# Layer 0's first norm, its values and its first queries and keys, made tile by tile of 128 features

## The chip, the core and the metric

The kernel runs on one core of one Trainium2 chip. The metric is the device time in microseconds of one execution of the whole program, the median of several runs; lower is better.

## The reference

256 tokens of 1024 features go through three layers: attention with a SwiGLU feed-forward, attention of another kind with a SwiGLU, and a convolution module with a convolutional feed-forward. Every sublayer is fed by a norm whose scale and shift come from a conditioning vector `c` through one large matrix (`ada_w`, 1024 x 6144 a layer).

```python
mod = (c_act @ ada_w[i] + ada_b[i])[:, None, :]
sh_a, sc_a, g_a, sh_f, sc_f, g_f = jnp.split(mod, 6, axis=-1)
h = rms_norm(x, norm_g[i, 0]) * (1.0 + sc_a) + sh_a
y = moba_attention(h, moba_w_qkv[i // 2], moba_w_o[i // 2], rel_bias)
x = x + g_a * rms_norm(y, norm_g[i, 1])
```

In layer 0 nothing can be projected before scale `sc_a` and shift `sh_a` are known. Each is a product of `c_act` with a 1024 x 1024 block of `ada_w`, 4 MB. The projections `h @ w_qkv` (1024 x 3072: queries, keys, values) follow.

## The kernel before

All weights stream from HBM once, in loads of 1 MB on SP's DMA queue (`load`, L74), into four buffers (`rawp`), and for the first three loads into tiles that other data uses later. A load can be issued when the last reader of its buffer is done. A weight unit is split into two pieces (`split`, L96): ACT copies it in the matrix engine's rounding (`h`, L108) and VectorE (DVE) subtracts that from the original (`l`, L110). Each product is three matmuls (`mm3`, L135 to L137). The activations `T` are split in the same way and stand with features on the partitions, in 8 tiles `k` of 128 features.

The first stretch of the program: `first_norm` (L284) loads the 8 MB of scale and shift in rows of 4 KB, multiplies them by `c_act` on the matrix engine (`quads`, L220), turns the two sums into columns, and scales the normed, transposed `x` by them. `project` (L207, first layer: `before=shifted`) makes the values V for all 256 tokens from four units of 1 MB. Then the loop of `attention` makes queries and keys for four pairs of heads, each from a unit of 1 MB (`cols_unit`, rows of 1 KB). While it does, the attention of the earlier heads is woven in (`step`): its first product is the scores matmul L615, which stands on the matrix engine's queue between the two blocks of pair 1's queries. Before that also stand the matmuls that turn the position bias (L375).

The other vectors of modulation are made in the background: `bg_step` takes a quarter of a vector (a load of 1 MB and two operations of 128x1024 on DVE, L202 and L204) at given places. The table `plans` says how many quarters a stage takes, over how many places, and how many places it leaves out first; layer 0's attention takes 12 quarters, and needs all of them at its end for the next norm.

A list scheduler sets the order in which the instructions stand on each engine's queue when the program is built; on the chip each queue runs strictly in that order.

## Time and profile before

| | us |
|---|---|
| median of 3 runs (lowest, highest) | 970.23 (968.81, 971.09) |
| profiled execution: first to last instruction | 967.0 |
| matrix engine (PE) busy | 928.9 |
| DVE busy | 767.5 |
| ACT busy | 495.1 |

The page gives the profiled execution's time from its first to its last instruction alone; the runs' median lies 3.2 us above it, which is what lies around the span. An engine is busy when one of its instructions runs; two matmuls overlap in the pipeline, so that PE's busy time says that it was fed, not that it was at its peak.

### The profile page before, as it was taken

To read this page: it belongs to the slowest core of one execution; us is meant where nothing else is said; L and a number is where in the kernel's file an instruction comes from. 1 tells how busy PE (TensorE), PEld (TensorE's weight loads), DVE (VectorE), ACT (ScalarE), POOL (GpSimd) and SP (SyncE) were. 2 spreads that over 40 slices of the span, in tenths; PEclk is the share of its full clock that TensorE was granted. 3 is DMA by queue.
4 is the path that set the end of the run, shared out by engine and by line. 5 is a ranking of instruction groups with operands and counts; after the bars stand their busy time and mean duration, and the time that the engine had idled before them with its cause. 6 is when DMAs were issued, how large, how long until landed. Compare 5 with 4: busy or idle time off the path is not lost.

```text
span 967.0 us, 17220 instructions
## 1 busy us (share of the span) xinstructions
PE 928.9 (96%) x6687; PEld 811.4 (84%) x6687; DVE 767.5 (79%) x1461; ACT 495.1 (51%) x870; POOL 51.2 (5%) x118
## 2 busy tenths in 40 slices
PE   5899999999999999999999999999999899999997
PEld 2579977998999879876799989987897779999996
DVE  1779977976878798887999878888777789977774
ACT  2355665543344445675634444555416755655552
POOL 2100000000000010122100000001000100000000
PEclk9999999999999999999999999999999999999999
DMA  9988885978879859673588899786747466975511
GB/s 349 390 318 293 316 283 176 322 283 317 282 272 382 300 185 348 225 259 106 167 285 320 311 345 336 275 303 204 269 113 201 142 208 226 302 231 188 175 45 44
DMA packets 141519, 244.06 MB, mean 252 GB/s; under 512 B 6662, under 2 KB 106174, under 8 KB 141438
## 3 DMA queue, kind: packets, MB, share of 16 engines
q1 hardware_dynamic: 140918, 241.64, 72.1%
q0 software_dynamic: 496, 1.31, 0.4%
q8 instruction: 52, 0.85, 0.4%
q14 instruction: 29, 0.24, 0.1%
q10 hardware_dynamic: 24, 0.01, 0.0%
HBM read 240.94 MB, written 2.01 MB: 251 GB/s over the span
## 4 chain that ended last, share of the span: by engine, by line
issue 44%; PE 30%; DVE 4%; POOL 4%; ACT 2%; DMA 1%; SPq 0%; DVEq 0%; POOLq 0%; ACTq 0%
PE up L137 5%; PE up L136 5%; PE up L135 5%; PE acc L135 4%; PE acc L137 4%; PE acc L136 4%; PE acc L851 1%; DVE l L110 1%; POOL rstd L480 1%; POOL var L478 1%; ACT h L108 1%; POOL orstd L652 1%; ACT junk L473 1%; POOL ovar L650 1%; DMA raw<-in_f_up_w_dram 1%
## 5 line engine op out<-in xcount | busy, mean ns | idle before, releaser
L110 DVE TENSOR_TENSOR l<-raw,h 128x512 fp32r<-128x512 f32 x548 | 354.7, 684 | 80.6 <-ACT h L108 78.2
L108 ACT ACTIVATE h<-raw 128x1024 fp32r<-128x1024 f32 x274 | 280.1, 1053 | 171.1 <-PE up L136 38.0
L137 PE MATMUL up<-th,l 128*128 128x256 f32 x640 | 181.7, 284 | 0.0
L136 PE MATMUL up<-tl,h 128*128 128x256 f32 x640 | 181.1, 283 | 0.0
L135 PE MATMUL up<-th,h 128*128 128x256 f32 x640 | 180.8, 282 | 0.0
L204 DVE SCALAR_TENSOR_TENSOR gemv<-raw,c_s,gemv 128x1024 f32<-128x1024 f32 x112 | 143.2, 1279 | 0.9
L135 PEld LDWEIGHTS up<-th,h 128*128 128x128 f32 x640 | 121.0, 189 | 2.0 <-DVE ml L747 0.4
L137 PEld LDWEIGHTS up<-th,l 128*128 128x128 f32 x640 | 120.7, 189 | 0.1
L136 PEld LDWEIGHTS up<-tl,h 128*128 128x128 f32 x640 | 120.4, 188 | 0.4
L135 PE MATMUL acc<-h,mh 128*128 128x512 f32 x232 | 91.6, 395 | 0.1
L136 PE MATMUL acc<-l,mh 128*128 128x512 f32 x232 | 90.9, 392 | 0.0
L137 PE MATMUL acc<-h,ml 128*128 128x512 f32 x232 | 90.5, 393 | 0.0
L137 PE MATMUL up<-oh,l 128*128 128x256 f32 x288 | 81.9, 284 | 0.0
L136 PE MATMUL up<-ol,h 128*128 128x256 f32 x288 | 81.7, 284 | 0.0
L135 PE MATMUL up<-oh,h 128*128 128x256 f32 x288 | 81.1, 282 | 0.0
L135 PE MATMUL acc<-th,h 128*128 128x256 f32 x256 | 75.1, 293 | 0.1
L137 PE MATMUL acc<-th,l 128*128 128x256 f32 x256 | 73.8, 288 | 0.2 <-DVE l L110 0.2
L136 PE MATMUL acc<-tl,h 128*128 128x256 f32 x256 | 72.7, 284 | 0.0
L135 PEld LDWEIGHTS up<-oh,h 128*128 128x128 f32 x288 | 54.6, 189 | 0.8
L136 PEld LDWEIGHTS up<-ol,h 128*128 128x128 f32 x288 | 54.2, 188 | 0.7
L137 PEld LDWEIGHTS up<-oh,l 128*128 128x128 f32 x288 | 54.4, 189 | 0.1
L135 PEld LDWEIGHTS acc<-h,mh 128*128 128x128 f32 x232 | 43.6, 188 | 11.1 <-issue 2.5
(230 smaller groups left out, 1663.7 us busy)
## 6 DMA issues: line engine op xcount, KB each, us to landing
raw<-in_ada_w_dram SPq DMA_DIRECT2D x46, 1024.0 KB
raw<-in_ffn_w_in_dram SPq DMA_DIRECT2D x36, 1024.0 KB
raw<-in_mod_w_dram SPq DMA_DIRECT2D x24, 1024.0 KB
raw<-in_ffn_w_out_dram SPq DMA_DIRECT2D x22, 1024.0 KB
raw<-in_f_up_w_dram SPq DMA_DIRECT2D x18, 1024.0 KB
raw<-in_moba_w_qkv_dram SPq DMA_DIRECT2D x12, 1024.0 KB
raw<-in_diff_w_qkv_dram SPq DMA_DIRECT2D x12, 1024.0 KB
raw<-in_f_down_w_dram SPq DMA_DIRECT2D x11, 1024.0 KB
```

Source lines behind the costliest of these rows:

```text
L108: newest["high"] = nc.scalar.activation(h, r, AF.Copy).ins
L110: newest["split"] = nc.vector.tensor_sub(l[:, k], r[:, k], h[:, k].bitcast(F32)).ins
L135: nc.tensor.matmul(ps, lh, rh, start=start, stop=False, skip_group_check=True)
L136: nc.tensor.matmul(ps, lh, rl, start=False, stop=False, skip_group_check=True)
L137: nc.tensor.matmul(ps, ll, rh, start=False, stop=stop, skip_group_check=True)
L204: nc.vector.scalar_tensor_tensor(t, src, c[:, k:k + 1], t, op0=ALU.mult, op1=ALU.add)
L473: nc.scalar.activation(junk, src, AF.Square, scale=1.0 / 32, accum_out=ss[:, i:i + 1])
L478: nc.gpsimd.tensor_scalar(v, ss[:, 0:1], ss[:, 1:2], EPS, op0=ALU.add, op1=ALU.add)
L480: nc.gpsimd.tensor_tensor(r, v, mhalf, op=ALU.pow)
L650: nc.gpsimd.tensor_scalar(var, ss, 1.0 / DH, EPS, op0=ALU.mult, op1=ALU.add)
L652: nc.gpsimd.tensor_tensor(rn, var, mhalf, op=ALU.pow)
L851: mm = nc.tensor.matmul(ps[32 * g:32 * g + 32, 0:P], lw[t][:, m, g, :], ur[:, g, 4 * m:4 * m + P], start=m == 0, stop=m == 7, tile_positio ...
```

## The change

Scale and shift of layer 0's first norm are made for 128 features at a time. For each of the 8 tiles one load of 1 MB takes the 128 columns of scale and the 128 of shift that belong to the tile: 2 x 1024 pieces of 512 bytes. The product with `c_act` is made on PE for tiles 0 to 2 (`FIRST_ON_PE`) and on DVE for tiles 3 to 7: one multiply and seven multiply-adds of 128x256 (new lines L337 and L339), then two matmuls with one column each (L342) and two small operations (L345, L347) that leave scale and shift as columns. ACT makes the tile of `T` with them (L349, L350), DVE its second piece (L351). As soon as a tile of `T` is there, its share of all values and of pair 0's queries and keys is added up in PSUM, 12 matmuls of 512 and 12 of 256 columns a tile. Pair 0's queries and keys come in two units with rows of 1 KB (`half_unit`). `x` is loaded first. The background's 12 quarters start in pair 1 (`plans`), 8 of them beside pairs 1 to 3 and 4 beside the output projection.

```diff
+    def first_columns():
...
+        rows = work.tile([24, P], F32, name="rowsm", tag="w")
+        w, b, c = jobs[0][0], jobs[0][1], jobs[0][5]
+        for i, v in enumerate((b[D:2 * D], b[0:D], jobs[0][3])):
+            nc.scalar.dma_start(rows[8 * i:8 * i + 8, :], v.rearrange("(k p) -> k p", p=P))
+        ps = tr.tile([P, 512], F32, name="tr")
+        nc.tensor.transpose(ps[:, 0:24], rows, ident[:24, :24])
+        col = one.tile([P, 24], F32, name="mcol")
+        nc.vector.tensor_copy(col, ps[:, 0:24])
+        nc.vector.tensor_scalar(col[:, 0:8], col[:, 0:8], 1.0, None, op0=ALU.add)
+        return col
...
+    def first_load(k):
+        w = jobs[0][0]
+        return load(lambda raw: [(raw[:, 1024 * i:1024 * i + 1024].rearrange("p (r n) -> p r n", r=8),
+                                  w[:, j * D + k * P:j * D + k * P + P].rearrange("(p r) n -> p r n", r=8))
+                                 for i, j in enumerate((1, 0))])
+    def first_tile(T, k, raw, col, on_pe):
+        c = jobs[0][5]
+        rows = raw.rearrange("p (j r n) -> p j r n", j=2, r=8)
+        g = work.tile([P, 2, P], F32, name="fgem", tag="w")
+        if on_pe:
+            ps = tr.tile([P, 512], F32, name="tr")
+            for r in range(8):
+                q = 32 * (r % 4)
+                nc.tensor.matmul(ps[q:q + 32, 0:256], c[:, r:r + 1].to_broadcast([P, 32]), rows[:, :, r, :],
+                                 start=r < 4, stop=r >= 4, tile_position=(0, q), skip_group_check=True)
+            nc.scalar.activation(g.rearrange("p j n -> p (j n)"), ps[:, 0:256], AF.Copy)
+        else:
+            nc.vector.tensor_scalar(g, rows[:, :, 0, :], c[:, 0:1], None, op0=ALU.mult)
+            for r in range(1, 8):
+                nc.vector.scalar_tensor_tensor(g, rows[:, :, r, :], c[:, r:r + 1], g, op0=ALU.mult, op1=ALU.add)
+        ps = tr.tile([P, 512], F32, name="tr")
+        for j in range(2):
+            nc.tensor.matmul(ps[:, j:j + 1], g[:, j, :], pick if on_pe else ones32[:, 0:1], start=True, stop=True,
+                             skip_group_check=True)
+        m = small.tile([P, 2], F32, name="fcols")
+        nc.vector.scalar_tensor_tensor(m[:, 0:1], ps[:, 0:1], col[:, k:k + 1], col[:, 16 + k:17 + k],
+                                       op0=ALU.add, op1=ALU.mult)
+        nc.vector.tensor_tensor(m[:, 1:2], ps[:, 1:2], col[:, 8 + k:9 + k], op=ALU.add)
+        v = work.tile([P, S], F32, name="fv", tag="w")
+        nc.scalar.activation(T[0][:, k, :], nb[:, k, :], AF.Identity, scale=m[:, 0:1], bias=m[:, 1:2])
+        nc.scalar.activation(v, nb[:, k, :], AF.Identity, scale=m[:, 0:1], bias=m[:, 1:2])
+        nc.vector.tensor_sub(T[1][:, k, :], v, T[0][:, k, :].bitcast(F32))
...
+    def first_project(w):
...
+        T = new_T("t")
+        col = first_columns()
+        turned = first_rows()
+        vals = [[acc.tile([P, 512], F32, name="acc") for _ in range(2)] for _ in range(2)]
+        qk = [up.tile([P, 512], F32, name="up") for _ in range(2)]
+        vw, qw = {}, {}
...
+        def values(k):
+            wh, wl = vw[k // 2][k % 2]
+            for h in range(2):
+                for n in range(2):
+                    sl = slice(512 * n, 512 * n + 512)
+                    mm3(vals[h][n], *tok(T, k, h), wh[:, sl], wl[:, sl], k == 0, k == NK - 1)
+        def heads(k):
+            wh, wl = (t[:, k % 2, :] for t in qw[k // 4][k // 2 % 2])
+            for i in range(2):
+                for b in range(2):
+                    sl = slice(256 * i + 128 * b, 256 * i + 128 * b + 128)
+                    mm3(qk[i][:, 256 * b:256 * b + 256], wh[:, sl], wl[:, sl], T[0][:, k, :], T[1][:, k, :],
+                        k == 0 and b == 0, k == NK - 1)
+        def tile_of(k):
+            first_tile(T, k, raws.pop(k), col, k < FIRST_ON_PE)
+        raws = {0: first_load(0)}
+        v0 = rows_load(w, 0, 2 * D)
+        raws[1] = first_load(1)
+        tile_of(0)
+        with tc.issue_after(turned):
+            make_c2()
+        vw[0] = split(v0, after=turned)
+        load_qk(0)
         for k in range(NK):
-            v = nb[:, k, :]
-            nc.vector.tensor_scalar(v, v, cols[0][:, k:k + 1], None, op0=ALU.mult)
...
+            if k + 2 < NK:
+                raws[k + 2] = first_load(k + 2)
+            if k + 1 < NK:
+                tile_of(k + 1)
+            if k % 2 == 0 and k + 2 < NK:
+                load_v(k // 2 + 1)
+            if k == 2:
+                load_qk(1)
+            values(k)
+            heads(k)
+        return T, qk, vals
...
@@ -661,14 +723,31 @@
     def attention(diff, T, w_qkv, w_o, first):
         v = big.tile([P, 2, D], F32, name="v")
-        for h, ps in project(T, w_qkv, 2 * D, ("oh", "ol"), before=first):
-            for n in range(2):
-                nc.scalar.activation(v[:, h, 512 * n:512 * n + 512], ps[n], AF.Copy)
+        pairs = []
+        scale = -float(DH // (2 if diff else 1)) ** -0.5
+        def pair(pq, pk):
+            q = two.tile([P, 2, S], F32, name="q")
+            nc.scalar.activation(q, pq.rearrange("p (b n) -> p b n", b=2), AF.Copy, scale=scale)
+            yield
...
+            nc.scalar.activation(kk, pk.rearrange("p (b n) -> p b n", b=2), AF.Copy)
+            pairs.append((q, kk))
         if first:
+            T, qk, vals = first_project(w_qkv)
+            for h, ps in enumerate(vals):
+                for n in range(2):
+                    nc.scalar.activation(v[:, h, 512 * n:512 * n + 512], ps[n], AF.Copy)
+            for _ in pair(*qk):
+                pass
             next(bias)
             lam_col()
+        else:
+            for h, ps in project(T, w_qkv, 2 * D, ("oh", "ol")):
+                for n in range(2):
+                    nc.scalar.activation(v[:, h, 512 * n:512 * n + 512], ps[n], AF.Copy)
         O = new_T("o")
...
             elif flight:
                 advance()
-        for i in range(4):
+        if first:
+            heads(0)
+        for i in range(len(pairs), 4):
             pq = acc.tile([P, 512], F32, name="acc")
...
             pk = acc.tile([P, 512], F32, name="acc")
+            made = pair(pq, pk)
...
+            next(made, None)
             heads(i)
         step()
...
     stages.append((2, 2, lambda T: conformer(T, a["a_pw1_w_2"][0], a["a_pw2_w_2"][0], a["a_pw2_b_2"][0])))
     stages.append((2, 5, lambda T: conv_ffn(T, a["f_up_w_2"][0], a["f_down_w_2"][0])))
```

On SP's queue (the program's start), before the change: the weights of scale, then of shift, then the units of V.

```order
L151 DMA c1_v_100<-in_c_dram 128x8
L80 DMA raw0_129<-in_ada_w_dram 128x2x1024
L80 DMA raw0_139<-in_ada_w_dram 128x2x1024
L80 DMA raw0_149<-in_ada_w_dram 128x2x1024
L301 DMA x_99<-in_x_dram 128x1024 x2
L80 DMA raw_161<-in_ada_w_dram 128x1024 x2
L80 DMA raw_230<-in_ada_w_dram 128x2x1024
...
L80 DMA raw_260<-in_ada_w_dram 128x1024 x2
L80 DMA raw_311<-in_moba_w_qkv_dram 128x2x1024
L80 DMA raw_335<-in_moba_w_qkv_dram 128x2x1024
```

And with the change (`8x128` is eight pieces of 128 numbers on each partition; `2x1024` a unit of V, `4x256` of pair 0):

```order
L299 DMA x_105<-in_x_dram 128x1024 x2
L81 DMA raw0_209<-in_ada_w_dram 128x8x128 x2
L81 DMA raw0_212<-in_moba_w_qkv_dram 128x2x1024
L81 DMA raw0_214<-in_ada_w_dram 128x8x128 x2
L81 DMA raw_249<-in_moba_w_qkv_dram 128x4x256 x2
L81 DMA raw_262<-in_ada_w_dram 128x8x128 x2
L81 DMA raw_286<-in_moba_w_qkv_dram 128x2x1024
L81 DMA raw_322<-in_ada_w_dram 128x8x128 x2
L81 DMA raw_370<-in_ada_w_dram 128x8x128 x2
L81 DMA raw_392<-in_moba_w_qkv_dram 128x2x1024
L81 DMA raw_404<-in_moba_w_qkv_dram 128x4x256 x2
L81 DMA raw_441<-in_ada_w_dram 128x8x128 x2
```

Tiles 0 to 3 of scale and shift are raw0_209, raw0_214, raw_262 and raw_322; tile 4 is raw_370; the last, raw_545, stands four loads further on. `x` has moved ahead of all weights, and the units of V and of pair 0 stand between the tiles.

On DVE's queue, where V is made, before the change: the second pieces of the weight units (L110) alternate with those of `T` (L341).

```order
L313 COPY col_276<-up_273 128x8
L341 SCALAR_TENSOR_TENSOR tl_121<-nb_113,col_276,th_120 128x256 x2
L110 TENSOR_TENSOR park_309<-raw_311,park_309 128x512 x2
L110 TENSOR_TENSOR park_310<-raw_311,park_310 128x512 x2
L341 SCALAR_TENSOR_TENSOR tl_121<-nb_113,col_276,th_120 128x256 x2
L110 TENSOR_TENSOR l_338<-raw_335,h_337 128x512 x2
L110 TENSOR_TENSOR l_343<-raw_335,h_342 128x512 x2
```

With the change, tile 4 (its sum is `fgem_444`): the splits of V's third unit (raw_392) and of pair 0's second (raw_404) stand inside its chain of multiply-adds.

```order
L337 TENSOR_SCALAR fgem_444<-raw_370,c1_s_108 128x256
L339 SCALAR_TENSOR_TENSOR fgem_444<-raw_370,c1_s_108,fgem_444 128x256
L351 TENSOR_TENSOR tl_141<-fv_388,th_140 128x256
L339 SCALAR_TENSOR_TENSOR fgem_444<-raw_370,c1_s_108,fgem_444 128x256
L112 TENSOR_TENSOR l_395<-raw_392,h_394 128x512 x2
L112 TENSOR_TENSOR l_400<-raw_392,h_399 128x512 x2
L339 SCALAR_TENSOR_TENSOR fgem_444<-raw_370,c1_s_108,fgem_444 128x256
L112 TENSOR_TENSOR l_408<-raw_404,h_407 128x512 x2
L112 TENSOR_TENSOR l_413<-raw_404,h_412 128x512 x2
L339 SCALAR_TENSOR_TENSOR fgem_444<-raw_370,c1_s_108,fgem_444 128x256 x4
L345 SCALAR_TENSOR_TENSOR fcols_456<-tr_453,mcol_148 128x1
```

And the end of tile 7, the last (`fgem_591`), with the change: a background vector's multiply-adds (`gemv_775`, now L208 and L210) and the split of pair 1's keys (raw_785) stand inside its chain.

```order
L208 TENSOR_SCALAR gemv_775<-raw_773,c1_s_108 128x1024
L339 SCALAR_TENSOR_TENSOR fgem_591<-raw_545,c1_s_108,fgem_591 128x256
L210 SCALAR_TENSOR_TENSOR gemv_775<-raw_773,c1_s_108,gemv_775 128x1024
...
L210 SCALAR_TENSOR_TENSOR gemv_775<-raw_778,c1_s_108,gemv_775 128x1024
...
L112 TENSOR_TENSOR l_788<-raw_785,h_787 128x512
L339 SCALAR_TENSOR_TENSOR fgem_591<-raw_545,c1_s_108,fgem_591 128x256
L112 TENSOR_TENSOR l_788<-raw_785,h_787 128x512
L345 SCALAR_TENSOR_TENSOR fcols_603<-tr_600,mcol_148 128x1
```

Where before no instruction of DVE stood between a load of scale or shift and the matmuls that read it, five of the eight tiles now pass through DVE's queue, in the order shown.

## Rows read from the trace of the kernel before

**Rows 1.** The page's head: span, and busy time of each engine.

```profile
span 967.0 us, 17220 instructions
PE 928.9 (96%) x6687; PEld 811.4 (84%) x6687; DVE 767.5 (79%) x1461; ACT 495.1 (51%) x870; POOL 51.2 (5%) x118
```

**Rows 2.** Windows: from:to, length, busy us (instructions) per engine, PEclk, DMA share, GB/s.

```profile
core 0: us, PE busy (x) PEld busy (x) DVE busy (x) ACT busy (x) POOL busy (x), PEclk, DMA share, GB/s
40.00:50.00 10.00, 10.00 (x44) 7.66 (x43) 8.55 (x12) 4.68 (x6) 0.00 (x0) 1.00 1.01 391
70.00:80.00 10.00, 10.00 (x87) 9.97 (x85) 8.57 (x16) 5.45 (x8) 0.00 (x0) 1.00 1.05 377
120.00:140.00 20.00, 19.74 (x101) 15.88 (x101) 15.01 (x40) 13.11 (x32) 0.92 (x2) 1.00 0.86 290
```

**Rows 3.** Timeline of the start, PE: start, us, instruction, idle before and what ended it.

```profile
6.96 1.93 PE L220 MATMUL acc<-raw,c_s 128*32 128x256 f32 x16 [6.96 <-DMA raw<-in_ada_w_dram]
...
17.10 1.97 PE L327 MATMUL tr<-ident,hn 128*128 128x128 f32 x8 [2.46 <-DVE hn L324]
...
28.26 0.64 PE L220 MATMUL acc<-raw,c_s 128*32 128x256 f32 x8 [0.63 <-DMA raw<-in_ada_w_dram]
29.45 0.44 PE L311 MATMUL up<-ident,row 128*128 128x128 f32 x2 [0.55 <-DVE row L306]
32.71 1.59 PE L135 MATMUL acc<-park,th 128*128 128x512 f32 x3 [2.83 <-ACT park L108]
```

**Rows 4.** Windows around the first matmuls of V.

```profile
33.00:34.00 1.00, 1.00 (x3) 0.81 (x3) 1.00 (x3) 1.00 (x3) 0.00 (x0) 0.50 1.02 406
...
37.00:38.00 1.00, 1.00 (x6) 0.82 (x5) 1.00 (x3) 0.17 (x1) 0.00 (x0) 1.00 0.98 365
```

**Rows 5.** Timeline from 55 us, PE without L135 to L137.

```profile
57.55 1.98 PE L375 MATMUL tr<-toep,stage 128*128 128x512 f32 x4
59.61 1.88 PE L375 MATMUL tr<-toep,stage 128*128 128x512 f32 x4
76.20 0.38 PE L615 MATMUL up<-kk,q 128*128 128x128 f32 x2
```

**Rows 6.** DMA from 18 to 24 us (rows of 4 KB): packets, MB, share of 16 engines.

```profile
DMA packets 629, 2.45 MB, mean 408 GB/s; under 512 B 32, under 2 KB 32, under 8 KB 629
...
q1 hardware_dynamic: 629, 2.45, 102.1%
```

**Rows 7.** DMA from 128 to 138 us (rows of 1 KB).

```profile
DMA packets 3551, 3.52 MB, mean 352 GB/s; under 512 B 110, under 2 KB 3551, under 8 KB 3551
...
q1 hardware_dynamic: 3551, 3.52, 109.3%
```

**Rows 8.** Groups by line and form: busy us, mean ns of one, idle before.

```profile
L837 DVE SCALAR_TENSOR_TENSOR z<-ud,dcol,z 128x256 f32<-128x256 f32 x60 | 24.2, 477 | 0.0
...
L108 ACT ACTIVATE park<-raw 128x1024 fp32r<-128x1024 f32 x12 | 12.3, 1052 | 8.3 <-DMA raw<-in_a_pw_w_dram 3.1 <-DMA raw<-in_ffn_w_in_dram 2.6 <-issue 2.1
...
L948 DVE TENSOR_TENSOR ml<-m,mh 128x256 fp32r<-128x256 f32 x22 | 9.2, 419 | 1.5 <-ACT mh L947 1.5
...
L340 ACT ACTIVATE th<-nb,col 128x256 fp32r<-128x256 f32 x8 | 3.6, 495 | 7.6 <-DVE col L313 7.6
...
L626 DVE SCALAR_TENSOR_TENSOR rl<-rs,nlam,sm 128x1 f32<-128x1 f32 x16 | 3.4, 213 | 0.2
...
L332 DVE TENSOR_SCALAR nb<-nb,col 128x256 f32<-128x256 f32 x8 | 2.2, 348 | 0.0
```

**Rows 9.** Timeline of DVE from 40 us.

```profile
41.03 2.50 DVE L110 TENSOR_TENSOR l<-raw,h 128x512 fp32r<-128x512 f32 x4 [1.86 <-ACT h L108]
...
43.85 0.74 DVE L202 TENSOR_SCALAR gemv<-raw,c_s 128x1024 f32<-128x1024 f32 x1
...
44.91 3.92 DVE L204 SCALAR_TENSOR_TENSOR gemv<-raw,c_s,gemv 128x1024 f32<-128x1024 f32 x3
...
64.35 0.15 DVE L395 TENSOR_TENSOR lamd<-lamx 128x1 f32<-128x1 f32 x1
```

**Rows 10.** Waits of SP's queue, 0 to 120 us: in total, times, longest.

```profile
SPq L80 <- DVE l L110: 31.5, 10, 4.7
SPq L80 <- DMA raw<-in_ada_w_dram: 11.5, 4, 3.7
```

More of the change, by code (lines that the diff above doesn't have):

```diff
@@ L1 @@
 import math
-from contextlib import ExitStack
+from contextlib import ExitStack, nullcontext
 import numpy as np
@@ L94, in parked, with split @@
         return rooms
-    def split(raw, blocks=False, rooms=None):
+    def split(raw, blocks=False, rooms=None, after=None):
         pieces = []
@@ L107, in split @@
                 h, l = (t.rearrange("p (k n) -> p k n", k=8) for t in (h, l))
-            newest["high"] = nc.scalar.activation(h, r, AF.Copy).ins
+            with tc.issue_after(after) if after else nullcontext():
+                newest["high"] = nc.scalar.activation(h, r, AF.Copy).ins
             for k in (slice(0, 4), slice(4, 8)) if blocks else (slice(0, 512), slice(512, 1024)):
@@ L144, in net @@
     nc.vector.memset(ones32, 1.0)
+    pick = one.tile([P, 1], F32, name="pick")
+    nc.gpsimd.memset(pick, 0.0)
+    for i in range(4):
+        nc.gpsimd.memset(pick[32 * i:32 * i + 1, :], 1.0)
     mhalf = one.tile([P, 1], F32, name="mhalf")
@@ L181, in load_quad, with mod_load @@
         return t
-    def mod_load(w, j, r, halved=False):
+    def mod_load(w, j, r):
         src = w[:, j * D:j * D + D].rearrange("(p k) n -> p k n", k=8)[:, 2 * r:2 * r + 2, :]
-        if halved:
-            return load(lambda raw: [(raw[:, 1024 * kk:1024 * kk + 1024], src[:, kk, :]) for kk in range(2)])
         return load(lambda raw: [(raw.rearrange("p (k n) -> p k n", k=2), src)])
@@ L215, in mod_finish @@
                           row.rearrange("(g r) n -> g r n", r=32)[:, 0, :])
-    def quads(ps, c, k, src, start, stop):
-        for q in range(4):
-            nc.tensor.matmul(ps[32 * q:32 * q + 32, 0:256], c[:, k:k + 1].to_broadcast([P, 32]),
-                             src[:, 256 * q:256 * q + 256], start=start, stop=stop,
-                             tile_position=(0, 32 * q), skip_group_check=True)
     def mod_vector(w, b, j, g, slot, c):
@@ new lines, in first_rows @@
+    def first_rows():
+        for h in range(2):
+            nc.sync.dma_start(x[:, h, :], a["x"][0, h * P:h * P + P, :])
+        for h in range(2):
+            ss = small.tile([P, 2], F32, name="ss")
+            src = halves(x[:, h, :])
+            for n in range(2):
+                squares(ss, n, src[n])
+            r = rstd_of(ss)
+            for n in range(2):
+                t = two.tile([P, 512], F32, name="hn")
+                nc.vector.tensor_scalar(t, src[n], r, None, op0=ALU.mult)
+                ps = tr.tile([P, 512], F32, name="tr")
+                for q in range(4):
+                    nc.tensor.transpose(ps[:, q * P:q * P + P], t[:, q * P:q * P + P], ident)
+                ins = nc.scalar.activation(nb[:, 4 * n:4 * n + 4, h * P:h * P + P],
+                                           ps.rearrange("p (k n) -> p k n", k=4), AF.Copy).ins
+        return ins
@@ L528, in rows_matmul, with project @@
             mm3(ps[n], lh, ll, wh[:, sl], wl[:, sl], k0 + i == 0, k0 + i == nk - 1)
-    def project(T, w, c0, tags=(), between=None, early=0, before=None):
+    def project(T, w, c0, tags=(), between=None, early=0):
         ps = [[acc.tile([P, 512], F32, name="acc") for _ in range(2)] for _ in range(2)]
@@ L534, in project @@
         for u in range(4):
-            if before:
-                before(u)
             units.append(rows_unit(w, 2 * u, c0, parked(*tags) if u == 0 else None))
@@ L696, in attention @@
             bg_step()
-            pv = pq.rearrange("p (b n) -> p b n", b=2)
-            q = two.tile([P, 2, S], F32, name="q")
-            nc.scalar.activation(q, pv, AF.Copy, scale=-float(DH // (2 if diff else 1)) ** -0.5)
             pk = acc.tile([P, 512], F32, name="acc")
+            made = pair(pq, pk)
+            next(made)
             cols_matmul(pk.rearrange("p (b n) -> p b n", b=2), T, cols_unit(w_qkv, D + 256 * i), step)
             bg_step()
-            kk = two.tile([P, 2, S], F32, name="kk")
-            nc.scalar.activation(kk, pk.rearrange("p (b n) -> p b n", b=2), AF.Copy)
-            pairs.append((q, kk))
+            next(made, None)
             heads(i)
@@ L977, in conv_ffn @@
         yield 1, banks[1]
-    T = new_T("t")
-    shifted = first_norm(T)
+    T = None
     bias = bias_tiles()
@@ L990, in net @@
         w_qkv, w_o = ((a["moba_w_qkv"][0], a["moba_w_o"][0]), (a["diff_w_qkv"][0], a["diff_w_o"][0]))[layer]
-        stages.append((layer, 2, lambda T, l=layer, q=w_qkv, o=w_o: attention(l == 1, T, q, o, None if l else shifted)))
+        stages.append((layer, 2, lambda T, l=layer, q=w_qkv, o=w_o: attention(l == 1, T, q, o, l == 0)))
         stages.append((layer, 5, lambda T, l=layer: swiglu(T, a["ffn_w_in"][l], a["ffn_w_out"][l], hooks[l])))
```

82 lines of the change are left out of this document (19 added, 63 removed).

## The prediction

> **What bounds the kernel now.** I read the page's head first: PE is busy for 929 of 967 us [rows 1], so that the kernel is a row of matmuls with few holes, and a change at its start counts by what it does to the moment at which that row is at a given matmul. The windows show the same by stretch: 44 matmuls of 512 columns in 10 us (0.227 us each) and 87 of 256 columns (0.115 us each), PE busy throughout [rows 2]. Then the timeline of the start. The first weights of scale land at 6.96 us, the last of shift at 28.26, and the first matmul of V starts at 32.71 [rows 3]. From there PE is fed. As the mark by which before and after compare I take the first scores matmul, L615 at 76.20 us [rows 5]: all of V, pair 0, half of pair 1's queries and the bias matmuls stand ahead of it in both programs. What is left to do on PE behind it is the same in both, so what the mark loses or gains goes through to the end, but for the background work (below).
>
> **What the change does, part by part.** It removes the wait of V for all 8 MB: the first tile's matmuls can start after `x`, one tile and one unit of V. By the loads below pair 0's first unit, whose copy stands ahead of the first tile of `T` on ACT, lands at 6.96 + 4.0 + 2.66 + 4.0 + 3.15 = 20.8 us; with 1.05 for that copy and 0.5 for the tile V starts near 22, 10 us sooner than 32.71. It also removes the 128 matmul records of L220, most of which lay in the wait for weights, and one background vector's work ahead of the mark. None of this is a gain by itself: V and pair 0 can't be finished before the last tile has landed, gone through DVE and been multiplied. So I follow the last tile.
>
> The loads. A load of 1 MB in rows of 4 KB takes (28.26 - 6.96) / 8 = 2.66 us [rows 3]. Pieces of 512 bytes in numbers like these don't occur before; I price them by a line through two rows. With rows of 4 KB a piece holds an engine for 1.021 x 16 x 6 us / 629 = 156 ns [rows 6], with rows of 1 KB 1.093 x 16 x 10 us / 3551 = 49.2 ns [rows 7]; the line through both gives 31.4 ns at 512 bytes, so that a tile (2048 pieces on 16 engines) takes 4.0 us, and a unit of 1 KB rows 3.15. The bounds: 2.66 us if only bytes count, 6.3 us if a piece costs no less than one of 1 KB. I take 4.0, since the two rows show that the piece has a part that doesn't shrink with its bytes. The Trainium skill (DMA: Bandwidth & Descriptors, Specifications) gives 512 bytes as the smallest transfer that still runs at line rate. By that rule a tile costs 2.66 us, and the sum below comes to +7 instead of +13; it is the second rival's page.
>
> On SP's queue `x` is first and lands about when the first MB did, 6.96. Up to tile 3, the first that goes through DVE, there follow four tiles (16.0), V's units 0 and 1 (5.3), a unit of pair 0 (3.15) and, from POOL's queue, the 1 MB of the bias table in rows of 1 KB (3.15), which is asked for earlier than before: tile 3 is there at 34.6 us.
>
> DVE's queue from there to the last multiply-add of tile 7, in the order printed above. Five tiles of one multiply (0.348) and seven multiply-adds (0.477) [rows 8] are 18.4 us, and 1.0 more since each waits for the one before (three in 3.92 us where one is 1.28 [rows 9]). 17 halves of weight splits at 0.625 (four in 2.50 [rows 9]) are 10.6. Five second pieces of `T` at 0.42 [rows 8] are 2.1; eight small column operations, 0.21 and 0.15 [rows 8, 9], 1.4; the background's four, 0.74 and three at 1.3 [rows 9], 4.6. Together 38.1 us of work; before the change DVE did only the splits and second pieces of it ahead of V's matmuls. The waits between: tiles 3 and 4 have nothing between their sum and their column operations, so DVE stands for the two matmuls with one column (0.25 us each, from eight transposes in 1.97 [rows 3], and the way there and back, 0.7 in all) twice, 1.4; V's third unit lands at 34.6 + 4.0 + 2.66 = 41.3, ACT's copy takes 1.05 [rows 8], and DVE, which would be there at 41.3, waits 1.05 with the rest of tile 4 queued behind it; V's fourth unit, whose buffer V's third gives back only after its split (such waits of SP's queue for L110 are 31.5 us in the first 120 already [rows 10]), costs another 0.6. That is 3.1, and the last multiply-add ends at 34.6 + 38.1 + 3.1 = 75.8 us. It is the splits and the background inside tile 7's chain that make this late: tile 7's own weights land near 59.
>
> Then tile 7's column: 0.7 for the matmuls, 0.4 for the small operations, 0.5 for ACT's tile (L340 [rows 8]); its matmuls start at 77.4. On PE before the mark: 12 x 0.227 + 12 x 0.115 = 4.1; three of the four bias matmuls, which before took 57.55 to 61.49 [rows 5], 2.95; 24 matmuls of pair 1's queries, 2.8. PE has stood idle for some 8 us by then (tile 6 starts near 64.7 and takes 4.1). After 2.83 us of idling the granted clock was at 0.50 for V's first matmuls and back at 1.00 some 3.3 us later [rows 3, 4], that is 1.2 instead of 2.4 GHz, so that these 3.3 us bring half: 1.65 more. The mark falls at 77.4 + 4.1 + 2.95 + 2.8 + 1.65 = 88.9, against 76.2: 12.7 us later.
>
> Behind the mark: four background quarters now stand beside the output projection, where none stood. A quarter is two operations of 1.28, together 10 us on DVE, which is busy for 15.0 of 20 us there [rows 2] and so has some 6 us free in the projection's 24. Hidden, it costs nothing; if the rest holds up the norm behind it, 4 us. I take 0.3, since the quarters come early in the projection, and keep 0 to 4. PE's earlier idling is behind the last tile's and adds nothing: tile 4 too stands behind the two splits and starts near 51, but tile 7 would come no sooner.
>
> The sum is 967.0 + 12.7 + 0.3 = 980.0 us of span; with the 3.2 by which the runs' median (970.2) lies above the profiled span, 983.
>
> **The rivals.** First, DVE's queue doesn't hold tile 7 and the early start pays: the loads never stop and each tile's column follows its landing. Then tile 7 lands at 6.96 + 8 x 4.0 + 4 x 2.66 + 2 x 3.15 + 3.15 = 59.0, its column takes 4.1 + 1.6, and the mark is at 64.7 + 9.85 = 74.6, 1.6 us earlier: 968.6, no change that can be told. To be faster it needs the cheap pieces too: 8 x 1.34 us less, the mark at 63.8 and the time 958. The point from which it decides: with cheap pieces tile 3 lands at 29.2, and DVE's 41 us would have to shrink below 33. The order speaks against it, since the splits and the background stand in the queue whatever lands; for it speaks only that DVE is idle in parts of the start now.
>
> Second, the pieces run at the rate of their bytes (2.66 a tile), DVE's queue as forecast. Tile 3 lands 5.4 us earlier, and so does the mark: +7.3, 977.6. The rule of the page cited above is this case; the two rows with pieces of 4 KB and 1 KB speak against it.
>
> Third, the pieces are dearer, up to 6.3 us a tile. Each of the eight then delays what follows, 2.3 us each, 18 us at most if nothing hides it: up to 1001. The prices of 4 KB and 1 KB fit no such step, but no row excludes it.
>
> Fourth, the background beside the projection holds up the norm: +4, 987.
>
> **How the numbers follow.** A difference under 0.2% (1.9 us) is what a measurement of this kernel can't tell from no change. The forecast (979 to 987) has 0.62, the cheap pieces (975 to 979) 0.14, the dearer ones or more waits, the background with them (987 to 1001), 0.14, the loads alone as limit (968 to 972) 0.03, and faster 0.07. The first two and the lower half of the third make the range, 975 to 994. So: faster 0.07, same 0.03, slower 0.90.
>
> **What would show it.** Right: V's first matmul near 22 us; DMA packets of 512 bytes near 31 ns of an engine; DVE busy from about 35 to 76 us with the new L339 and the splits in turn; PE idle ahead of tile 4's and most of all tile 7's column matmuls, released by DVE's L339, with a clock of 0.5 behind it; the first scores matmul near 89 us; the stretches from 200 us on shifted by as much and else alike. Wrong: tile 7's column matmuls before 66 us (then DVE's queue was not the bound), PE idle ahead of the tiles released by DMA (then the pieces are the bound), or the gap at the mark not found at the end (then something behind it gave time back).

## The result and the profile after

| | before | after |
|---|---|---|
| median of 4 runs (lowest, highest), us | 969.5 (968.5, 971.1) | 983.7 (983.2, 984.3) |
| ratio, 95% interval | | 1.0145 (1.0131 to 1.0159) |
| profiled execution, first to last instruction, us | 967.0 | 981.4 |

The change makes the kernel 1.5% slower. The page's head, to be laid beside [rows 1]:

```profile
span 981.4 us, 17196 instructions
PE 934.4 (95%) x6636; PEld 818.1 (83%) x6636; DVE 782.5 (80%) x1506; ACT 501.7 (51%) x881; POOL 52.7 (5%) x122
```

DVE has 15 us more work, PE 5.5, and the span is 14.4 longer. The timeline of PE says where this arises: V's first matmul, the column matmuls (L342) of tiles 4 and 7, tile 7's first matmul of V, the first scores matmul (the mark), and the first norm's transposes.

```profile
21.51 0.77 PE L139 MATMUL acc<-h,th 128*128 128x512 f32 x1 [1.15 <-ACT th L349]
...
48.61 0.80 PE L342 MATMUL tr<-ones,fgem 128*128 128x1 f32 x4 [4.33 <-DVE fgem L339]
...
74.23 1.01 PE L342 MATMUL tr<-ones,fgem 128*128 128x1 f32 x4 [3.66 <-DVE fgem L339]
...
76.25 1.33 PE L139 MATMUL acc<-h,th 128*128 128x512 f32 x1
...
88.13 0.39 PE L677 MATMUL up<-kk,q 128*128 128x128 f32 x2
...
160.56 0.63 PE L576 MATMUL tr<-ident,hn 128*128 128x128 f32 x4 [0.67 <-DVE hn L572]
```

V starts 11.2 us sooner than in [rows 3], and the mark comes 11.9 us later than in [rows 5]. The waits of PE in the first 100 us (total, times, longest) name DVE's new chain ahead of all else but the bias table of the program's start:

```profile
PE tr L423 <- DMA stage<-in_hot_dram: 10.5, 1, 10.5
PE tr L342 <- DVE fgem L339: 9.0, 3, 4.3
PE acc L139 <- ACT th L349: 3.2, 3, 1.1
```

DVE's timeline of tile 7 shows what the chain waits for: not its weights (no wait for a load stands in it), but what else stands in the queue.

```profile
64.37 0.35 DVE L337 TENSOR_SCALAR fgem<-raw,c_s 128x256 f32<-128x256 f32 x1
64.63 0.68 DVE L112 TENSOR_TENSOR l<-raw,h 128x512 fp32r<-128x512 f32 x1
...
66.96 0.74 DVE L208 TENSOR_SCALAR gemv<-raw,c_s 128x1024 f32<-128x1024 f32 x1
67.62 0.47 DVE L339 SCALAR_TENSOR_TENSOR fgem<-raw,c_s,fgem 128x256 f32<-128x256 f32 x1
68.02 1.27 DVE L210 SCALAR_TENSOR_TENSOR gemv<-raw,c_s,gemv 128x1024 f32<-128x1024 f32 x1
...
73.70 0.48 DVE L339 SCALAR_TENSOR_TENSOR fgem<-raw,c_s,fgem 128x256 f32<-128x256 f32 x1
74.10 0.68 DVE L112 TENSOR_TENSOR l<-raw,h 128x512 fp32r<-128x512 f32 x1
75.28 0.22 DVE L345 SCALAR_TENSOR_TENSOR fcols<-tr,mcol 128x1 f32<-128x1 f32 x1 [0.50 <-PE tr L342]
```

Eight operations that would take some 4 us alone, as in tile 6, take 9.8. Last, the DMA from 29 to 32 us, when only pieces of 512 bytes are on the way (packets, MB, share of 16 engines):

```profile
q1 hardware_dynamic: 1731, 0.87, 113.9%
```

1.139 x 16 x 3 us / 1731 is 31.6 ns a piece. The share above 100% says that pieces overlap on an engine: counted by what arrives, 1731 pieces in 3 us, the 2048 pieces of a tile take 3.55 us.

### The profile page after: what moved, and what is told of

The parts are those of the page before. It is cut to its first block, busy times and chain, and to the rows that moved or that the text cites. A ratio compares the mean times of both kernels' runs of the same rounds, so it can differ in the third digit from the quotient of the medians.

```text
span 981.4 us, 17196 instructions
## 1 busy us (share of the span) xinstructions
PE 934.4 (95%) x6636; PEld 818.1 (83%) x6636; DVE 782.5 (80%) x1506; ACT 501.7 (51%) x881; POOL 52.7 (5%) x122
## 4 chain that ended last, share of the span: by engine, by line
issue 43%; PE 39%; DVE 5%; POOL 3%; DMA 3%; ACT 3%; SPq 2%; DVEq 0%; POOLq 0%; ACTq 0%
PE acc L139 6%; PE acc L141 6%; PE acc L140 6%; PE up L141 6%; PE up L140 5%; PE up L139 5%; DVE l L112 2%; DMA raw<-in_moba_w_qkv_dram 2%; SPq L81 1%; PE acc L929 1%; ACT h L110 1%; POOL rstd L544 1%; PE up L703 1%; POOL var L542 1%; PE up L677 1%
## 5 line engine op out<-in xcount | busy, mean ns | idle before, releaser
L110 ACT ACTIVATE h<-raw 128x1024 fp32r<-128x1024 f32 x276 | 282.6, 1054 | 166.2 <-PE up L140 39.9
L141 PE MATMUL up<-th,l 128*128 128x256 f32 x672 | 190.8, 284 | 0.0
L140 PE MATMUL up<-tl,h 128*128 128x256 f32 x672 | 190.4, 283 | 0.0
L139 PE MATMUL up<-th,h 128*128 128x256 f32 x672 | 190.0, 283 | 0.0
L210 DVE SCALAR_TENSOR_TENSOR gemv<-raw,c_s,gemv 128x1024 f32<-128x1024 f32 x112 | 143.2, 1278 | 0.6
L139 PEld LDWEIGHTS up<-th,h 128*128 128x128 f32 x672 | 127.5, 190 | 2.5 <-DVE ml L825 0.4
L140 PEld LDWEIGHTS up<-tl,h 128*128 128x128 f32 x672 | 126.6, 188 | 0.8
L141 PEld LDWEIGHTS up<-th,l 128*128 128x128 f32 x672 | 126.9, 189 | 0.1
L139 PE MATMUL acc<-th,h 128*128 128x256 f32 x224 | 66.1, 295 | 0.0
L140 PE MATMUL acc<-tl,h 128*128 128x256 f32 x224 | 64.1, 286 | 0.0
L141 PE MATMUL acc<-th,l 128*128 128x256 f32 x224 | 64.0, 286 | 0.0
L817 ACT ACTIVATE sg<-up 128x256 f32<-128x256 f32 x44 | 16.8, 381 | 73.0 <-PE up L141 42.6
```

Source lines behind the costliest of these rows:

```text
L110: newest["high"] = nc.scalar.activation(h, r, AF.Copy).ins
L139: nc.tensor.matmul(ps, lh, rh, start=start, stop=False, skip_group_check=True)
L140: nc.tensor.matmul(ps, lh, rl, start=False, stop=False, skip_group_check=True)
L141: nc.tensor.matmul(ps, ll, rh, start=False, stop=stop, skip_group_check=True)
L210: nc.vector.scalar_tensor_tensor(t, src, c[:, k:k + 1], t, op0=ALU.mult, op1=ALU.add)
L817: nc.scalar.activation(g, ps[:, 0:256], AF.Silu)
```

## The experiments

The theory: DVE's queue sets when tile 7 is ready, and what the mark loses goes through to the end. Its rivals: the loads set the pace; the four quarters beside the output projection hold up the norm. A third came up in the middle: what counts is how much of the background is left behind the mark. All runs are compared with runs of the kernel before on the same chip. "Stretch" is the time from the mark to the first norm's transposes, 68.3 us before, 72.4 after.

**1. No sums on DVE** (`sums_on_pe`).

```diff
-FIRST_ON_PE = 3
+FIRST_ON_PE = 8
```

> All eight tiles' sums on the matrix engine instead of three; the five chains of multiply-adds leave DVE's queue. If DVE's queue sets when the last tile is ready, the loads take its place: tile 7's weights land near 58 us (tile 3 at 33.1 in the changed kernel, then four tiles at 4.0, two units of V at 2.66 and one of pair 0 at 3.15), its sum (1.0), copy (0.35) and column (1.6) let its matmuls start near 61, and the first scores matmul falls at 71 to 75 us instead of 88.1; the time is 967 to 972 us, about that of the kernel before. If the loads in pieces of 512 bytes already set the pace, the mark stays within 3 us of 88.1 and the time at 981 to 984.

Measured: 976.2 us, 1.0056 (1.0036 to 1.0075) of before, between the two expected ranges. Timeline of PE: tile 7's column matmuls, the mark, the first norm.

```profile
61.08 0.50 PE L342 MATMUL tr<-pick,fgem 128*128 128x1 f32 x4
...
75.74 0.39 PE L677 MATMUL up<-kk,q 128*128 128x128 f32 x2
...
151.46 0.87 PE L576 MATMUL tr<-ident,hn 128*128 128x128 f32 x3 [5.74 <-DVE hn L572]
```

Tile 7 is ready at 61, as expected if DVE's queue was the bound, and the mark comes 12.4 us sooner: the rival of the loads falls. But the end gains only 7.4. PE now stands 5.7 us ahead of the norm, waiting for DVE, so that a mark even 0.5 us ahead of the kernel before leaves the time 5.5 us above it. In the windows from 148 to 158 us, in and behind this idling, the granted clock is 0.50 (1.2 GHz) as well.

**2. The price of the pieces** (`rows4k`).

```diff
-        ... w[:, j * D + k * P:j * D + k * P + P].rearrange("(p r) n -> p r n", r=8))
+        rows = w[:, (1 - k // 4) * D:(2 - k // 4) * D].rearrange("(p r) n -> p r n", r=8)
+        ... rows[:, 2 * (k % 4) + i, :]) for i in range(2)])
```

> The changed kernel with the eight tiles' loads of 1 MB read as whole rows of 4 KB, so that the sums are made of other columns than the tile's; instructions and their order stay. If a piece of 512 bytes costs 31 to 32 ns, each 1 MB lands 1.34 us sooner, tile 3 some 5.4 us sooner, and with DVE's queue as the bound from tile 3 on the mark and the end come 4 to 6 us earlier: 978 to 980 us. If DVE is so far behind that the landing of tile 3 doesn't matter, or if the pieces run at the rate of their bytes, nothing changes: mark within 1 us of 88.1, 982.5 to 984.5.

Measured: 980.7 us, 1.0098 (1.0077 to 1.0119), just above the expected 978 to 980. Tile 3's first operation on DVE; tile 7's column matmuls and the mark on PE:

```profile
30.14 0.35 DVE L336 TENSOR_SCALAR fgem<-raw,c_s 128x256 f32<-128x256 f32 x1
```

```profile
71.56 0.76 PE L341 MATMUL tr<-ones,fgem 128*128 128x1 f32 x4 [3.81 <-DVE fgem L338]
...
84.56 0.39 PE L676 MATMUL up<-kk,q 128*128 128x128 f32 x2
```

Tile 3 starts 3.65 us sooner than at 33.79 and the mark comes 3.57 sooner. Not all of the 3.65 passes through DVE's queue: tile 7's column matmuls start at 71.56 instead of 74.23, 2.7 sooner. The other 0.9 is the clock, which is at 0.50 for 3.4 us around tile 7 here and for 6.8 in the changed kernel (experiment 7). That tile 3 gains 3.65 and not 5.4 fits its landing, which the trace's semaphore updates put at 30.04 instead of 33.70: four tiles of 3.55 us instead of 2.57 (1 MB at the 408 GB/s of [rows 6]) are 3.9.

**3. The background out of tile 7's chain** (`late_bg`).

```diff
-    plans = ((12, 10, 0), ...
+    plans = ((12, 8, 2), ...
```

> The changed kernel with the background's first two places left out: its four multiply-adds of 4.6 us leave tile 7's chain on DVE, three halves of splits (0.625 each) come into it, 8 quarters follow beside pairs 2 and 3 and 4 beside the projection. If DVE's queue sets the mark, tile 7's matmuls and the mark come 2 to 4 us sooner (84 to 86), and the time is 980 to 982. If tile 7 is held by its splits' loads, the mark stays within 1 us of 88.1.

Measured: 988.8 us, 1.0195 (1.0171 to 1.0219). Tile 7's column matmuls, mark and norm on PE:

```profile
71.73 0.61 PE L342 MATMUL tr<-ones,fgem 128*128 128x1 f32 x4 [1.06 <-DVE fgem L339]
...
82.79 0.39 PE L677 MATMUL up<-kk,q 128*128 128x128 f32 x2
...
162.82 1.94 PE L576 MATMUL tr<-ident,hn 128*128 128x128 f32 x8 [6.36 <-DVE hn L572]
```

The mark gains 5.3 us, more than expected, and the end loses 4.1 (985.5 against 981.4 of span). Neither theory had that. Tile 7's columns come 2.5 us sooner, as expected of the chain; the other 2.8 of the mark is the clock, which stays at 1.00 here (experiment 7). The chain of tile 7 is only half of the matter: the work taken out of it comes back at the norm.

**4. The four quarters beside the projection, taken away and put in** (`bg_pairs_only`, `before_four_proj`, `before_bg_proj`).

```diff
-    plans = ((12, 10, 0), ...      # the changed kernel
+    plans = ((12, 6, 0), ...
```

> The changed kernel with all 12 quarters in the six places beside pairs 1 to 3, none beside the output projection. By the forecast (quarters beside the projection are hidden) the time stays within 0.6 us of 983.7. If the quarters there are what the end lost beyond the mark (14.4 against 11.9 us), it is 1.5 to 2.5 us faster: 981 to 982. The mark stays at 88.1 in both cases, since the first quarters stand where they stood.

Measured: 981.6 us, 1.0112 (1.0091 to 1.0132), in the expected range of the rival. The timeline says otherwise:

```profile
86.48 0.38 PE L677 MATMUL up<-kk,q 128*128 128x128 f32 x2
...
157.30 0.96 PE L576 MATMUL tr<-ident,hn 128*128 128x128 f32 x5 [0.86 <-DVE hn L572]
```

1.65 of the 2.1 us that the span gains (979.3) lie ahead of the mark, where both programs have the same order on PE, DVE and ACT (experiment 7 comes back to this). Behind the mark there is 0.45 to be had at most, so the place of the quarters is not what the end lost.

In the kernel before, the quarters of its ten places were spread anew, with the first six as they were:

```diff
+    quarters = [0, 0, 2, 2, 1, 1, 1, 1, 0, 0, 0, 0, 1, 1, 1, 1]
```

> The kernel before with the same quarters in the first six places (2, 2, 1, 1, 1, 1), none beside pairs 2 and 3's last four, and the last four beside the output projection: the start's order stays, mark 76.2. By the forecast the four are hidden: 969.5 to 971. If they hold up the norm, PE waits for DVE ahead of the first norm's transposes by 2 us or more (0.7 before) and the time is 2 to 7 us longer, 972 to 977.

Measured: 970.2 us, 0.9995 (0.9986 to 1.0004); mark 76.63, first norm 145.03, PE's wait there 1.1 us. Four quarters beside the projection are hidden, as the forecast had it.

A first try left out the first four places instead, `(12, 12, 4)`:

> The kernel before with the background's first four places left out, so that of its 12 quarters four stand beside the output projection as in the changed kernel. By the forecast they are hidden there and the time stays within 0.5 us of before (969.3 to 970.3). If they hold up the norm behind the projection, it is 1.5 to 4 us slower (971 to 974), and the norm's first transposes come that much later behind the mark.

It gave 982.3 us, 1.0119 (1.0096 to 1.0142), and tells little: with the loads gone from the start, the scheduler put the bias matmuls (L375) ahead of the last product of shift, and PE waited 10.5 us for their table.

```profile
36.25 2.04 PE L375 MATMUL tr<-toep,stage 128*128 128x512 f32 x2 [10.49 <-DMA toep<-biasrows]
```

**5. How much is left behind the mark.** The same stretch in all these kernels, beside the background's operations on DVE (`gemv`) that fall in it:

| kernel | mark | first norm | stretch, us | gemv in it, us | PE idle in it, us |
|---|---|---|---|---|---|
| before | 76.20 | 144.50 | 68.3 | 14.8 | 0.9 |
| before_four_proj | 76.63 | 145.03 | 68.4 | 14.8 | 1.1 |
| bg_pairs_only | 86.48 | 157.30 | 70.8 | 19.4 | 1.5 |
| after | 88.13 | 160.56 | 72.4 | 19.4 | 0.7 |
| rows4k | 84.56 | 157.22 | 72.7 | 19.4 | 1.0 |
| sums_on_pe | 75.74 | 151.46 | 75.7 | 24.5 | 5.7 |
| late_bg | 82.79 | 162.82 | 80.0 | 29.1 | 8.2 |

An operation that is under way at an end of the stretch is counted whole; in the kernel before, one ends 0.1 us behind the mark, and 13.6 us lie wholly behind it. The rows behind the column of `gemv`, of `after` and of `late_bg` (busy us and mean ns of one):

```profile
L210 DVE SCALAR_TENSOR_TENSOR gemv<-raw,c_s,gemv 128x1024 f32<-128x1024 f32 x14 | 17.9, 1278 | 0.0
L208 DVE TENSOR_SCALAR gemv<-raw,c_s 128x1024 f32<-128x1024 f32 x2 | 1.5, 746 | 0.0
```

```profile
L210 DVE SCALAR_TENSOR_TENSOR gemv<-raw,c_s,gemv 128x1024 f32<-128x1024 f32 x21 | 26.9, 1280 | 0.1
L208 DVE TENSOR_SCALAR gemv<-raw,c_s 128x1024 f32<-128x1024 f32 x3 | 2.2, 748 | 0.0
```

From 14.8 to 29.1 us left, the stretch grows by 11.7: 0.8 us for each. The windows of the stretch (before, after, sums on PE) show that this is not one mechanism.

```profile
76.20:144.50 68.30, 67.42 (x471) 59.91 (x470) 58.86 (x146) 44.32 (x104) 1.95 (x4) 1.00 0.85 296
```

```profile
88.13:160.56 72.43, 71.76 (x490) 62.49 (x489) 62.17 (x147) 42.85 (x102) 3.02 (x4) 1.00 0.76 259
```

```profile
75.74:151.46 75.72, 69.98 (x491) 62.00 (x489) 70.30 (x158) 45.39 (x104) 5.76 (x6) 0.98 0.86 299
```

With the sums on PE, DVE is busy for 70.3 of 75.7 us and PE stands idle for 5.7 of them: there the deferred work holds PE up. After the change DVE is busy for 62.2 of 72.4 us and PE idle for no more than before; the stretch is longer there because PE does 19 matmuls more in it.

Two runs put this to the test in the kernel before, one with less of the background ahead of the mark, one with more. `before_defer` has `quarters = [0, 0, 0, 0, 1, 1, 1, 1, 2, 2, 2, 2, 0, 0, 0, 0]`, and its bias matmuls behind the last of L220:

> The kernel before with the same 12 quarters later: none in the four places of V, then 1, 1, 1, 1, 2, 2, 2, 2 beside the four pairs, none beside the projection; the matmuls of the bias are kept behind the last product of scale and shift, as they stood. In the six kernels looked at so far the stretch from the first scores matmul to the first norm's transposes grew by some 0.8 us for each us of the background's DVE operations that was left for it (before: 14.8 left, 68.3 long; the changed kernel 19.4 and 72.4; with its first places left out 29.1 and 80.0). If that is a cost of deferring and not of the new code, some 5 us more are left here (about 20), the stretch grows to 72 to 73.5 and the time to 973 to 976. If DVE has room behind the mark in the kernel before, it stays at 970 to 971.

Measured: 978.8 us, 1.0100 (1.0083 to 1.0116), above the expected 973 to 976. 20.7 us are left, the stretch is 72.0 (mark 80.41, norm 152.40), as expected; PE is idle for 2.4 us more of it than before and has eight matmuls more, so that here deferring does cost waits. The rest of the loss is 4.2 us at the mark; a wait for the bias table, which the edit didn't keep away, stands ahead of it:

```profile
37.46 2.05 PE L380 MATMUL tr<-toep,stage 128*128 128x512 f32 x2 [7.14 <-DMA toep<-biasrows]
```

The profiled execution was 4.7 us slower than the median; it lost some 6 us more between 668 and 778 us, far behind this stretch.

The other way, `before_sooner`, is `(12, 8, 2)` for `(12, 10, 2)` in the kernel before:

> The kernel before with its 12 quarters over 8 places instead of 10: 2, 2, 2, 2, 1, 1, 1, 1, so that 16 instead of 13 of the background's operations stand on DVE's queue ahead of the first scores, 3.9 us of work. If each us that is left behind the mark costs 0.8 in the kernel before too, the stretch from the mark to the first norm shrinks by some 3 us and the time falls to 966 to 968 if the mark stays. If DVE and the loads have no room ahead of the mark (DVE is busy for 8.5 of 10 us there, the DMA engines throughout), the mark comes later by as much as the stretch shrinks: 969 to 972.

Measured: 978.8 us, 1.0087 (1.0073 to 1.0101): slower by 8, outside both expectations. PE waits for weights that now stand behind the quarters (waits from 60 to 102 us):

```profile
PE acc L135 <- ACT h L108: 2.5, 1, 2.5
PE acc L137 <- DVE l L110: 1.4, 3, 0.9
```

These waits are half of the loss. Only 9.7 us are left behind the mark, yet the stretch is 73.9 us long. The mark itself has moved in the order: 24 matmuls of pair 1's queries, 2.8 us at 0.115 each, stand behind it that stood ahead of it. Counted from the same matmul as before, the mark would be near 81.6 and the stretch 71.1, still 2.8 longer than before with less left. So 0.8 us a us is a line through kernels with different limits, not a law by which hurrying would gain.

**6. Towards a better kernel** (`pe_pairs_only`, `pe_pairs_turn`, `pe_bg_sooner`), all with the sums on PE. First `(12, 6, 0)` as well:

> All eight sums on the matrix engine, and all 12 quarters in the six places beside pairs 1 to 3, none beside the output projection. With the sums alone the mark came at 75.7 us, 0.5 before that of the kernel before, but the end 7.0 later than its end: PE stood 5.7 us ahead of the first norm, waiting for DVE. If it is the quarters beside the projection that hold DVE up there, that wait shrinks below 1.5 us, the mark stays within 1 us of 75.7 and the time is 968 to 971 us. If it is the norm's place behind the weight splits whatever the background does, the wait and the time stay: 975 to 977.

Measured: 978.6 us, 1.0079 (1.0066 to 1.0093). The wait at the norm is gone (1.1 us), the time is not: stretch 77.3 with the same 24.5 us left, and PE idle for 6.1 us of it. The waits are now spread over the pairs. So the place beside the projection is not what costs. Nor does the amount alone set the stretch: with 24.5 us left it is 75.7, 77.3 and, in the next kernel, 80.3.

Then the bias buckets' matmul behind the transposes of `x`:

```diff
...
+        with tc.issue_after(newest["turn"]):
+            nc.tensor.matmul(ps[:NH, 0:384], tab, hot, start=True, stop=True)
...
```

> The same, and the small matmul of the bias buckets, for whose table PE's queue waits until 11.2 us, stands behind the 16 transposes of x instead of ahead of them. From 30 us on PE is busy throughout in the kernel with the sums on PE, so its start sets the mark as long as the loads don't: V's first matmul falls 3 to 6 us sooner than 22.3, the mark to 71 to 73 and the time 2 to 5 us below that of the kernel without this edit, 965 to 967.5, faster than the kernel before. If the loads or the copies of the first weights set V's start, it moves by less than 1.5 us, the mark stays near 75 and the time within 1.5 us of the other.

Measured: 983.1 us, 1.0127 (1.0104 to 1.0150), above both expected ranges. V's first matmul came at 22.75, no sooner: the table, asked for later in the program, landed at 16.1 instead of 11.2, and the sum of tile 0 stands behind it. The mark came at 79.07 and the stretch is 80.3; why both are longer than in the kernel without this edit was not followed up.

Last, four quarters beside tiles 6 and 7:

```diff
+            if k >= NK - 2:
+                bg_step()
...
+    plans = ((12, 8, 0), ...
```

> All eight sums on the matrix engine, and the first four quarters already beside tiles 6 and 7 (then 2, 2, 1, 1, 1, 1 beside pairs 1 to 3, none beside the projection). With the sums alone 24.5 us of the background's DVE operations were left behind the mark and the first norm's transposes came at 151.5. If what is deferred sets that moment, some 8 to 10 us fewer are left, PE's wait ahead of the norm (5.7) shrinks below 2, the transposes come at 144 to 148 and the time is 967 to 973 us. If PE's own added work (eight sums, 32 matmuls with one column) or the loads of pair 1, which now stand behind four more quarters, hold it up instead, it stays at 975 or above.

Measured: 977.1 us, 1.0072 (1.0060 to 1.0084). The wait at the norm shrinks to 1 us, but the transposes come at 153.2. Of the background 22.0 us are left, 2.5 fewer than with the sums alone and not 8 to 10; but the first scores matmul (69.97) stands ahead of the bias matmuls and of 24 of pair 1's here, so that mark and stretch can't be laid beside the others. The window from 70 us on shows PE short of work and the DMA engines half idle at first; the waits from 60 to 110 us name the background's own sums (L231) first, then the copies of weights that now stand behind the quarters, as the rival had it:

```profile
70.00:80.00 10.00, 8.16 (x35) 4.43 (x36) 8.61 (x20) 5.71 (x9) 0.00 (x0) 0.83 0.49 174
```

```profile
PE tr L231 <- DVE gemv L210: 2.7, 2, 1.8
PE acc L139 <- ACT h L110: 1.0, 1, 1.0
```

None of the three beats the kernel before.

**7. The clock at tile 7** (`warm7`).

```diff
...
+        if k == NK - 1:
+            for _ in range(14):
+                with tc.issue_after(warm or newest["mm"]):
+                    warm = nc.tensor.transpose(ps[:, P:2 * P], ident, ident).ins
...
```

> The changed kernel with 14 transposes of a constant (3.3 us) on PE's queue between tile 6's last matmul and tile 7's column matmuls, where it stands idle for 3.7 us; they feed nothing, and all other orders stay. In the changed kernel the granted clock is 0.5 for 6.8 us around tile 7, twice what the forecast counted. If the idling before tile 7 is what lowers it, the clock stays at 1.0 there, the mark comes 2 to 3.4 us sooner (84.7 to 86) and the end 0.5 to 3.4 sooner, since DVE's background behind the mark doesn't move. If the clock falls all the same, mark and end stay within 0.7 us of 88.1 and 983.7.

Measured: 982.8 us (982.2 to 986.2), 1.0145 (1.0130 to 1.0160): no difference that can be told. The mark came at 87.27, 0.9 sooner, between the two expectations. The 14 transposes took 1.7 us and not 3.3, so PE still stood idle for 1.8. The windows from 74 us, first of after, then of this kernel; the granted clock is the third figure from the end (0.50 is 1.2 GHz, 1.00 is 2.4):

```profile
74.00:76.00 2.00, 1.77 (x5) 1.35 (x6) 1.50 (x5) 0.40 (x2) 0.00 (x0) 0.50 0.95 356
76.00:78.00 2.00, 2.00 (x5) 1.14 (x4) 2.00 (x4) 1.29 (x3) 0.00 (x0) 0.50 0.93 314
78.00:80.00 2.00, 2.00 (x7) 1.55 (x6) 1.97 (x5) 0.84 (x2) 0.00 (x0) 0.60 1.06 364
```

```profile
74.00:76.00 2.00, 1.96 (x7) 1.13 (x8) 1.90 (x5) 1.10 (x3) 0.00 (x0) 0.91 0.96 360
76.00:78.00 2.00, 2.00 (x6) 1.22 (x6) 1.97 (x4) 1.07 (x2) 0.00 (x0) 0.50 0.89 275
78.00:80.00 2.00, 2.00 (x8) 1.63 (x7) 2.00 (x4) 1.01 (x2) 0.00 (x0) 0.74 1.07 369
```

Work at half clock shrinks from some 5 us to 3.4. From tile 7's columns to the mark it is 13.3 us instead of 13.9 (13.0 in `bg_pairs_only`, whose clock fell for as short a time without any help). So that much of the clock is worth 0.6 to 0.9 us. What it is with no fall at all stands in the trace of `late_bg`, where PE waited only 1.06 us ahead of tile 7's columns. The same matmuls from there to the mark (one bias matmul stands sooner), first after, then in `late_bg`:

```profile
74.23:88.13 13.90, 13.85 (x61) 10.28 (x62) 9.68 (x19) 9.90 (x16) 0.00 (x0) 0.81 1.00 358
```

```profile
71.73:82.79 11.06, 11.06 (x61) 8.60 (x62) 4.33 (x14) 9.87 (x17) 0.00 (x0) 1.00 0.56 190
```

The whole fall costs the changed kernel 2.8 us ahead of the mark.

## Why the prediction was right

| step | forecast | measured |
|---|---|---|
| V's first matmul | 22 | 21.5 |
| a piece of 512 bytes, ns | 31.4 | 31.6 |
| a tile's load, us | 4.0 | 3.55 |
| tile 3 on DVE | 34.6 | 33.8 |
| tile 7's last multiply-add ends | 75.8 | 74.2 |
| tile 7's matmuls of V start | 77.4 | 76.25 |
| lost to the clock at tile 7 | 1.65 | 2.8 |
| the mark | 88.9 | 88.1 |
| lost at the mark | 12.7 | 11.9 |
| lost behind it | 0.3 | 2.5 |
| lost in all, span | 13.0 | 14.4 |
| time | 983 | 983.7 |

**How near the number came** is in part luck. What the mark lost was put 0.8 too high and what lies behind it 2.2 too low. The time is nearer than the loss because 3.2 us were added to the span for what lies around it. In both kernels that is 1.8: the profiled executions took 968.81 and 983.23 us with spans of 967.0 and 981.4. The other 1.4 of the 3.2 is by how much the profiled execution before was faster than the median of its runs.

**The loads.** The line through [rows 6] and [rows 7] met the price of a piece; the load of a tile, taken as 128 such prices one after another, was put at 4.0 us and is 3.55, since pieces overlap on an engine. The rule of the Trainium skill (DMA: Bandwidth & Descriptors, Specifications) that 512 bytes still run at line rate doesn't hold in this trace: eight pieces take 253 ns of an engine where one of 4 KB takes 156. Experiment 2 shows what that is worth here: 10.0 us above the kernel before instead of 14.2.

**DVE's queue.** Shown by experiments 1 and 2 from both sides: without the chains the mark is 12.4 us sooner, and of 3.65 us by which tile 3 is earlier 2.7 arrive at tile 7's columns. The forecast's 41.2 us from tile 3 to the end of tile 7 were 40.4. The waits in it were others than I named. For the copies of V's third unit DVE didn't wait; it waited 3.3 us for the column matmuls, 1.6 of them at tile 5, where PE was late itself.

**The clock.** The term was 3.3 us at half clock, 1.65 lost. PE worked for 5.4 us at half clock (1.2 GHz), 2.0 of them ahead of tile 7's matmuls of V, where the forecast had none; by `late_bg`, at 1.00 throughout, 2.8 were lost in all. These matmuls still started 1.15 us sooner than forecast, since the multiply-adds were done 1.6 sooner, and that covered it.

**Behind the mark.** Here the step was off: "What is left to do on PE behind it is the same in both ... but for the background work", and of that work it counted the four quarters beside the projection, at 0.3. Their place is indeed nearly free (experiment 4). What it left out is that the changed kernel reaches the mark with 8 of the background's operations done on DVE, and the one before with 13: 4.6 us more are left (5.8 with only what lies wholly behind the mark), and one vector's eight sum matmuls (L231, 0.12 us each, so 1.0 us) with them. The stretch grew by 4.1. PE's timeline at the norm, before and after:

```profile
144.50 1.29 PE L512 MATMUL tr<-ident,hn 128*128 128x128 f32 x8 [0.62 <-DVE hn L508]
...
155.03 0.63 PE L512 MATMUL tr<-ident,hn 128*128 128x128 f32 x4 [0.67 <-DVE hn L508]
```

```profile
160.56 1.23 PE L576 MATMUL tr<-ident,hn 128*128 128x128 f32 x8 [0.67 <-DVE hn L572]
162.78 0.50 PE L139 MATMUL up<-park,th 128*128 128x512 f32 x1 [0.99 <-ACT th L579]
...
169.59 1.29 PE L576 MATMUL tr<-ident,hn 128*128 128x128 f32 x8 [0.28 <-DVE hn L572]
```

In the stretch the changed kernel also does 11 matmuls of the output projection more than before ahead of the norm, 2.5 us. That is order, and 1.5 of it comes back by the second group of transposes: the first is 16.1 us later than before, the second 14.6, the end 14.4. The other 1.0 doesn't: PE waits 0.99 us for ACT's `th` where the kernel before has those 11 matmuls to do.

The windows from the mark to the end say whether the deferred work held PE up:

```profile
76.20:967.00 890.80, 868.58 (x6307) 768.74 (x6305) 722.68 (x1381) 463.83 (x821) 42.67 (x96) 1.00 0.71 244
```

```profile
88.13:981.40 893.27, 871.04 (x6315) 769.32 (x6313) 725.19 (x1381) 460.66 (x817) 44.21 (x96) 1.00 0.71 242
```

PE is idle for 22.2 us in both, so that other waits are shorter by as much, and busy for 2.5 more after the change. What was lost behind the mark is thus no longer waiting for DVE, and the 0.8 of experiment 5 doesn't explain it. About 1.0 of it is the eight sum matmuls; the other 1.5 of busy time stays open.

**The rivals.** The first (DVE's queue doesn't hold tile 7) is excluded in the changed kernel; experiment 1 made it true by force, and even then the time was 5.5 us above that of before, where the rival had 968.6. The second and third fall with 31.6 ns. The fourth, +4 for the quarters at the norm, falls too: PE waits 0.67 us for DVE there in the changed kernel and 0.62 before. The norm becomes the place of the loss only where more is left for DVE, in experiments 1 and 3.
